# A two-layer decoder trunk on one core: norm parameters and embedding inputs loaded from GpSimd's queue

## The chip, the cores and the metric

The kernel runs on one core of one Trainium2 chip. The metric is the device time of one execution in microseconds; the lower the better. The core has five engines with a queue of instructions each: TensorE (PE in the profile, with its weight loads as PEld), VectorE (DVE), ScalarE (ACT), GpSimd (POOL) and SyncE (SP), which here only issues loads and stores.

## The reference

Two layers over 512 tokens of width 1024 in float32. Layer 0 mixes tokens with a Mamba-2 SSD, layer 1 with an HGRN2; then both do the same:

```python
def sq_relu_mlp(h, w1, w2):
    a = jax.nn.relu(h @ w1)
    return (a * a) @ w2
...
h = layer_norm(DEEPNORM_ALPHA * x + mix, ln_g[i, 0], ln_b[i, 0])
h = layer_norm(DEEPNORM_ALPHA * h + sq_relu_mlp(h, mlp_w1[i], mlp_w2[i]), ln_g[i, 1], ln_b[i, 1])
x = h + jax.nn.sigmoid(h @ ple_w_gate[i]) * (p[i] @ ple_w_proj[i])
```

`w1` is 1024 x 4096, `w2` 4096 x 1024, `ple_w_gate` 1024 x 1024, and the embedding inputs `p[i]` are 512 x 256.

## The kernel before, in words

All tokens stay on the core. Every large product is made of three matmuls with operands that are split into a high and a low part. A weight of 128x1024 is loaded from SP's queue into one of **three `raw` buffers** (`unit`, L107), ScalarE casts it into a `whi` buffer (L114) and VectorE subtracts that into a `wlo` buffer (L116); there are six of each. The `raw` buffer is free for the next load when VectorE is done.

The MLP runs in five groups (`PERIODS`). Groups 0 to 3 make hidden tiles ("T": 24 matmuls of 128x512, then ReLU at L523 and square at L525 on ScalarE, into tiles `a` and `b` of the pool `w4`, two buffers each). `half_blocks` splits pairs of hidden tiles into blocks (casts L355 on ScalarE, subtractions L356 and sums L360 to L364 on VectorE). Groups 1 to 4 multiply the blocks of the group before by `w2` with Strassen's seven products ("Q", 24 matmuls each) in `block_product`. Some products take weights straight from `raw` buffers, the others sums of four loads that `weight_sums` makes in eight buffers `r` (loads L376, sums L382 to L388). A product fills two PSUM banks, py0 and py1 or two of the pool `pj`, and VectorE adds each to `acc` (L466; in group 4's last products L462, which also sums rows for the norm). In group 4 the order is a11, s3, s2, a22, s1, a12, s4; its norm (`layer_norm`, L204 to L215) follows the fifth and the last product. During groups 1 to 3 `sums_ahead` also prepares gate weights and writes them to `pre`.

At the start of group 4 `norm_blocks` calls `ln_params`, which loads the norm's two rows, broadcast to all partitions, into an `a` and a `b` tile. Then the embedding inputs are loaded into a `raw` buffer (L543), and split by ScalarE (L545) and VectorE (L546) into another `a` and `b` tile; the gate products read these after the MLP. The two mixers' norms call `ln_params` too (`norm`).

A scheduler of the framework sets the order of each engine's instructions, from the program's order and priorities (`tc.high_priority`); buffers go round in that order. A queue works in order, so an instruction that waits for a buffer holds those behind it. The names in the rows: `wlo<-raw,whi` is what is written, then what is read; a number behind a name is the buffer's allocation.

Of the kernel before, what the change touches and what calls it, by code (L numbers as in the profile page):

```python
# [9 lines left out]
F32R = mybir.dt.float32r  # L10
# [5 lines left out]
P = 128  # L16
T = 512
NCH = 4
D = 1024
# [22 lines left out]
def trunk(ctx: ExitStack, tc, a):  # L42
    nc = tc.nc
    pool = lambda name, bufs, **kw: ctx.enter_context(tc.tile_pool(name=name, bufs=bufs, **kw))
    cpool = pool("consts", 1)
    raws = pool("raws", RAWS)
# [4 lines left out]
    w4 = pool("w4", 2)  # L51
# [8 lines left out]
    def nm(s):  # L60
        uid[0] += 1
        return f"{s}_{uid[0]}"

    def mk(p, shape, tag, dt=F32, **kw):
        return p.tile(list(shape), dt, tag=tag, name=nm(tag), **kw)

    def f32(t):
        return t.bitcast(F32)
# [34 lines left out]
    def unit(src, lead=LEAD):  # L103
        n = src.shape[1]
        with tc.high_priority(offset=lead):
            raw = mk(raws, [P, 1024], "raw")
            nc.sync.dma_start(raw[:, :n], src)  # L107
        return split(raw[:, :n], lead)
# [83 lines left out]
    def ln_params(i):  # L192
        g = mk(w4, [P, D], "a")
        b = mk(w4, [P, D], "b")
        nc.sync.dma_start(g, a["ln"][2 * i : 2 * i + 1, :].to_broadcast([P, D]))
        nc.sync.dma_start(b, a["ln"][2 * i + 1 : 2 * i + 2, :].to_broadcast([P, D]))
        return g, b

    def layer_norm(c, gb, sums, junk):
# [74 lines left out]
    def norm(i, junk=lambda: tmp("sg", [P, T])):  # L274

        gb = ln_params(i)
        h_s = Split(8)
        sums = mk(sm, [P, NCH, 2], "lnsum")

        def chunk(c):  # L280
            with tc.high_priority(offset=SOON if c < 2 or i % 2 == 0 else 0):
                marks["norm", i] = layer_norm(c, gb, sums, junk)

        def turned(c):
            marks["turned", i] = transpose_split(acc[:, c, :], h_s, c)

        return h_s, chunk, turned, sums
# [4 lines left out]
    def norm_blocks(i):  # L292

        gb = ln_params(i)
        sums = mk(sm, [P, NCH, 2], "lnsum")
        blk = {n: mk(b8, [P, 2, 4, 256], "b8", F32R) for n in ("a11", "a12", "a22")}
# [128 lines left out]
    def ready(dst, n):  # L425

        us = []
        for u in range(2):
            with tc.high_priority(offset=LEAD):
                hi = mk(whip, [P, 1024], "whi", F32R)  # L430
                nc.sync.dma_start(f32(hi), dst[n, u, 0])
                lo = mk(wlop, [P, 1024], "wlo", F32R)
                nc.sync.dma_start(f32(lo), dst[n, u, 1])
            us.append((hi, lo))
        return us
# [50 lines left out]
    def mlp_and_gate(layer, h_s, last, turns=()):  # L486
# [48 lines left out]
        for g, period in enumerate(PERIODS):  # L535
            if g < 4:
                tiles = hidden(g)
            if g > 0:
                if g == 4:
                    blk, after, turned, sums, later = norm_blocks(2 * layer + 1)  # L540
                    p_s = (mk(w4, [P, 2, T], "a", F32R), mk(w4, [P, 2, T], "b", F32R))
                    praw = mk(raws, [P, 1024], "raw")
                    nc.sync.dma_start(praw, a[f"pT_{layer}"].rearrange("p k t -> p (k t)"))  # L543
                    praw = praw.rearrange("p (k t) -> p k t", k=2)
                    nc.scalar.copy(p_s[0], praw)  # L545
                    nc.vector.tensor_sub(p_s[1], praw, f32(p_s[0]))  # L546
                w = [[[w2[8 * g - 8 + 4 * i + 2 * j + u] for u in range(2)] for j in range(2)] for i in range(2)]
                products = block_product(w, blocks.pop(g - 1), SUMS[g - 1], g == 1, *((after, sums) if g == 4 else ()))
            for n, op in enumerate(period):
                next(tiles if op == "T" else products)  # L550
                if 0 < g < 4 and (op == "Q" or n == 1):
                    next(ahead, None)
                if g == 4:
                    for _ in ahead:
                        pass
# [64 lines left out]
        f = [unit(v) for v in wb[0][0]]  # L620
# [4 lines left out]
        f = [unit(v) for v in wb[1][0]]  # L625
# [8 lines left out]
        f = ready(pre, 2)  # L634
# [9 lines left out]
        f = ready(pre, 1)  # L644
# [4 lines left out]
        f = ready(pre, 3)  # L649
# [5 lines left out]
        f = ready(pre, 0)  # L655
# [7 lines left out]
        f = [unit(v) for v in wb[1][1]]  # L663
# [273 lines left out]
    with tc.manual_schedule(engines={mybir.EngineType.PE}):  # L937
# [8 lines left out]
        for k in range(1, 9):  # L946
            i, j = 2 * k, 2 * k + 1
# [47 lines left out]
    out_project(a["wso"][12:16], ys[3], False, *after, scale=rms_group(3, bank(psm, "pm")), spread=True)  # L995
    begin("mlp0")
    x_s, late = mlp_and_gate(0, h_s, False, [lambda c=c: after[1](c) for c in (2, 3)])
    begin("hgrn")

# [367 lines left out]
    out_project(a["who"][4:8], halves[1], False, *after)  # L1367
    begin("mlp1")
    mlp_and_gate(1, h_s, True)
    phase[1].__exit__(None, None, None)  # L1370

# [118 lines left out]
```

## Time and profile before

| what | value |
|---|---|
| median of 3 runs | 1406.96 us (1405.97 to 1407.67) |
| profiled execution: its own time, its span | 1406.46 us, 1404.7 us |
| granted TensorE clock | 1.00 |
| busy: PE, PEld | 1397.1 us (99%), 1167.6 us (83%) |
| busy: DVE, ACT, POOL | 1078.4 us (77%), 775.8 us (55%), 2.4 us |
| SP's DMA queue (q1): bytes, share of 16 engines | 196.59 MB, 41.1% |

Times in the rows are microseconds from the span's start. A row of the timeline gives start, duration, engine, line, operation, what is written and read, and in brackets the idle time before it with what ended it; "x2" is two in one row. SPq is SP's DMA queue: its time is that of issuing, not of the transfer.

### The profile page before, as it was taken

What the parts mean: (1) busy time and instruction counts of PE and PEld (TensorE: products, weight loads), DVE (VectorE), ACT (ScalarE), POOL (GpSimd) and SP (SyncE); (2) the same over time, 40 slices, a digit from 0 to 9 for tenths busy, and PEclk for the clock granted to TensorE, in tenths of its full rate; (3) what the DMA queues carried; (4) which work ended last, traced back from release to release, by engine and by line L of the source; (5) the groups of instructions that cost most, each with busy time, mean ns of one, the idle gap of its engine ahead of it and who ended that gap; (6) DMA issues with size and microseconds to landing.
All of it is one profiled execution on the core that took longest, in us unless ns stands there. A gap on an engine that the chain in (4) does not pass through costs nothing.

```text
span 1404.7 us, 20463 instructions
## 1 busy us (share of the span) xinstructions
PE 1397.1 (99%) x7957; PEld 1167.6 (83%) x7957; DVE 1078.4 (77%) x1780; ACT 775.8 (55%) x1165; POOL 2.4 (0%) x11
## 2 busy tenths in 40 slices
PE   9999999999999999999999999999999999999998
PEld 7888888888988888887888888888898888888787
DVE  7998877696867879679885775776785787778886
ACT  7886666573554555455564446465455464544563
POOL 0000000000000000000000000000000000000000
PEclk9999999999999999999999999999999999999999
DMA  8424333323354764653473321222173656646264
GB/s 296 158 99 135 105 106 120 105 91 106 132 183 143 238 219 162 212 194 135 134 288 120 106 91 67 86 94 73 61 255 114 213 177 223 217 151 210 97 243 155
DMA packets 66817, 214.68 MB, mean 153 GB/s; under 512 B 7712, under 2 KB 8352, under 8 KB 66592
## 3 DMA queue, kind: packets, MB, share of 16 engines
q1 hardware_dynamic: 57504, 196.59, 41.1%
q10 hardware_dynamic: 9216, 16.78, 3.3%
q8 instruction: 62, 1.02, 0.3%
q14 instruction: 35, 0.29, 0.1%
HBM read 194.41 MB, written 18.94 MB: 152 GB/s over the span
## 4 chain that ended last, share of the span: by engine, by line
PE 90%; DVE 5%; DMA 2%; ACT 1%; issue 1%; DVEq 0%; ACTq 0%; SPq 0%
PE pj L120 23%; PE pj L122 23%; PE pj L121 23%; PE py L120 5%; PE py L121 5%; PE py L122 5%; DMA r<-in_w 2%; DVE wlo L116 2%; PE py L880 1%; PE py L1147 1%; PE py L882 1%; DVE b L356 1%; DMA raw<-in_w 1%; PE pt L863 0%; DVE acc L466 0%
## 5 line engine op out<-in xcount | busy, mean ns | idle before, releaser
L116 DVE TENSOR_TENSOR wlo<-raw,whi 128x1024 fp32r<-128x1024 f32 x222 | 269.5, 1221 | 170.6 <-ACT whi L114 169.0
L114 ACT CAST whi<-raw 128x1024 fp32r<-128x1024 f32 x222 | 232.7, 1050 | 288.2 <-PE pj L121 147.9
L120 PE MATMUL pj<-b,whi 128*128 128x512 f32 (+1 forms) x1000 | 379.6, 380 | 0.0
L121 PE MATMUL pj<-b,whi 128*128 128x512 f32 (+1 forms) x1000 | 377.3, 377 | 0.0
L122 PE MATMUL pj<-b,wlo 128*128 128x512 f32 (+1 forms) x1000 | 377.3, 377 | 0.0
L122 PEld LDWEIGHTS pj<-b,wlo 128*128 128x128 f32 x1000 | 188.2, 188 | 34.7
L121 PEld LDWEIGHTS pj<-b,whi 128*128 128x128 f32 x1000 | 188.2, 188 | 34.3
L120 PEld LDWEIGHTS pj<-b,whi 128*128 128x128 f32 x1000 | 187.9, 188 | 34.2
L122 PE MATMUL pj<-whi,b 128*128 128x512 f32 x530 | 206.0, 389 | 0.0
L120 PE MATMUL pj<-whi,b 128*128 128x512 f32 x496 | 196.1, 396 | 0.2 <-DVE cv L753 0.2
L121 PE MATMUL pj<-wlo,b 128*128 128x512 f32 x496 | 193.1, 390 | 0.0
L122 PEld LDWEIGHTS pj<-whi,b 128*128 128x128 f32 x530 | 99.5, 188 | 20.7 <-DVE b L1342 0.2
L114 ACT CAST whi<-r 128x1024 fp32r<-128x1024 f32 x64 | 67.2, 1053 | 88.3 <-PE pj L121 67.7
L120 PEld LDWEIGHTS pj<-whi,b 128*128 128x128 f32 x496 | 93.1, 188 | 20.7 <-issue 0.7
L121 PEld LDWEIGHTS pj<-wlo,b 128*128 128x128 f32 x496 | 93.2, 188 | 18.5
L120 PE MATMUL py<-whi,b 128*128 128x512 f32 x256 | 100.5, 393 | 2.2 <-DVE acc L466 2.2
L122 PE MATMUL py<-whi,b 128*128 128x512 f32 x256 | 99.7, 389 | 0.0
L121 PE MATMUL py<-wlo,b 128*128 128x512 f32 x256 | 99.6, 389 | 0.0
L116 DVE TENSOR_TENSOR wlo<-r,whi 128x1024 fp32r<-128x1024 f32 x64 | 77.7, 1219 | 27.6 <-ACT whi L114 26.8
L120 PEld LDWEIGHTS py<-whi,b 128*128 128x128 f32 x256 | 48.1, 188 | 12.8 <-DVE acc L466 3.0
L122 PEld LDWEIGHTS py<-whi,b 128*128 128x128 f32 x256 | 48.0, 188 | 10.1
L121 PEld LDWEIGHTS py<-wlo,b 128*128 128x128 f32 x256 | 48.1, 188 | 9.8
(375 smaller groups left out, 1934.4 us busy)
## 6 DMA issues: line engine op xcount, KB each, us to landing
raw<-in_w SPq DMA_DIRECT2D x112, 512.0 KB, 3.7
r<-in_w SPq DMA_DIRECT2D x64, 512.0 KB, 4.2
raw<-in_wssd SPq DMA_DIRECT2D x38, 512.0 KB, 3.9
a<-csd SPq DMA_DIRECT2D x16, 512.0 KB, 3.7
raw<-in_wso SPq DMA_DIRECT2D x16, 512.0 KB, 3.8
pre<-sg ACTq DMA_DIRECT2D x32, 256.0 KB, 4.8
whi<-pre SPq DMA_DIRECT2D x16, 512.0 KB, 5.4
wlo<-pre SPq DMA_DIRECT2D x16, 512.0 KB, 6.3
```

The lines of the kernel that those rows point to most:

```text
L114: nc.scalar.copy(hi[:, :n], f)
L116: nc.vector.tensor_sub(lo[:, :n], f, f32(hi[:, :n]))
L120: nc.tensor.matmul(out, sh, mh, start=start, stop=False, **kw)
L121: nc.tensor.matmul(out, sh, ml, start=False, stop=False, **kw)
L122: marks["pe"] = nc.tensor.matmul(out, sl, mh, start=False, stop=stop, **kw)
L356: nc.vector.tensor_sub(lo, f, f32(hi))
L880: nc.tensor.matmul(yd[64 * r : 64 * r + 64, sl], xdt[:, c, r, :], m[:, r, sl], start=True, stop=c == 0)
L882: nc.tensor.matmul(yd[64 * r : 64 * r + 64, sl], pv[:, c - 1, r, :], ecs[:, r, (c - 1) * P : c * P], start=False, stop=True,)
L1147: nc.tensor.matmul(ps[r][32 * b : 32 * b + 32, base + n * c : base + n * c + n], kk[r][:, ts], moving(r, 4 * c + b), start=True, stop=True,)
```

## The change

The norm parameters' two loads are issued from GpSimd's queue in place of SP's, for all four norms. The embedding inputs' load is issued from GpSimd's queue too, and the code of that load and its split stands behind the third product of group 4, where it stood at the group's start.

```diff
     def ln_params(i):
         g = mk(w4, [P, D], "a")
         b = mk(w4, [P, D], "b")
-        nc.sync.dma_start(g, a["ln"][2 * i : 2 * i + 1, :].to_broadcast([P, D]))
-        nc.sync.dma_start(b, a["ln"][2 * i + 1 : 2 * i + 2, :].to_broadcast([P, D]))
+        nc.gpsimd.dma_start(g, a["ln"][2 * i : 2 * i + 1, :].to_broadcast([P, D]))
+        nc.gpsimd.dma_start(b, a["ln"][2 * i + 1 : 2 * i + 2, :].to_broadcast([P, D]))
         return g, b
...
                 if g == 4:
                     blk, after, turned, sums, later = norm_blocks(2 * layer + 1)
-                    p_s = (mk(w4, [P, 2, T], "a", F32R), mk(w4, [P, 2, T], "b", F32R))
-                    praw = mk(raws, [P, 1024], "raw")
-                    nc.sync.dma_start(praw, a[f"pT_{layer}"].rearrange("p k t -> p (k t)"))
-                    praw = praw.rearrange("p (k t) -> p k t", k=2)
-                    nc.scalar.copy(p_s[0], praw)
-                    nc.vector.tensor_sub(p_s[1], praw, f32(p_s[0]))
...
             for n, op in enumerate(period):
                 next(tiles if op == "T" else products)
+                if (g, n) == (4, 2):
+                    p_s = (mk(w4, [P, 2, T], "a", F32R), mk(w4, [P, 2, T], "b", F32R))
+                    praw = mk(raws, [P, 1024], "raw")
+                    nc.gpsimd.dma_start(praw, a[f"pT_{layer}"].rearrange("p k t -> p (k t)"))
+                    praw = praw.rearrange("p (k t) -> p k t", k=2)
+                    nc.scalar.copy(p_s[0], praw)
+                    nc.vector.tensor_sub(p_s[1], praw, f32(p_s[0]))
```

SP's queue around the start of group 4 in layer 0, before. `in_pT` is the embedding inputs, `in_ln` the norm parameters; `r` are the loads for sums; raw_5602 and raw_5608 are the weights of the group's product with a11.

```order
L107 DMA raw_5531<-in_w_0 128x1024
L376 DMA r_5589<-in_w_0 128x1024
L376 DMA r_5592<-in_w_0 128x1024
L543 DMA raw_5574<-in_pT 128x1024
L376 DMA r_5596<-in_w_0 128x1024
L376 DMA r_5599<-in_w_0 128x1024
L107 DMA raw_5602<-in_w_0 128x1024
L107 DMA raw_5608<-in_w_0 128x1024
L195 DMA a_5563<-in_ln 128x1024
L107 DMA raw_5808<-in_w_0 128x1024
L107 DMA raw_5814<-in_w_0 128x1024
L196 DMA b_5564<-in_ln 128x1024
```

The same place of SP's queue after the change; the weights of the product with a11 are raw_5596 and raw_5602 here.

```order
L107 DMA raw_5531<-in_w_0 128x1024
L376 DMA r_5583<-in_w_0 128x1024
L376 DMA r_5586<-in_w_0 128x1024
L107 DMA raw_5596<-in_w_0 128x1024
L376 DMA r_5590<-in_w_0 128x1024
L376 DMA r_5593<-in_w_0 128x1024
L107 DMA raw_5602<-in_w_0 128x1024
L107 DMA raw_5808<-in_w_0 128x1024
L107 DMA raw_5814<-in_w_0 128x1024
L107 DMA raw_5848<-in_w_0 128x1024
```

The first of these weights now stands where the embedding inputs stood, ahead of the last two `r` loads. POOL's queue of the same stretch after the change, where before the change stood only the fill:

```order
L548 DMA raw_5708<-in_pT 128x1024
L195 DMA a_5563<-in_ln 128x1024
L196 DMA b_5564<-in_ln 128x1024
L85 MEMSET pad_6410 128x32
```

The embedding inputs now wait for the `raw` buffer that raw_5531 leaves; the norm's two loads wait for the same readers of their buffers as before.

VectorE's queue at the change from group 3 to group 4, before (py_850 and py_851 are the banks py0 and py1 with group 3's last product; pj_5650 is the first bank of group 4's product with s3):

```order
L466 TENSOR_TENSOR acc_94<-pj_5344,acc_94 128x512
L116 TENSOR_TENSOR wlo_5684<-r_5592,whi_5682 128x1024
L466 TENSOR_TENSOR acc_94<-py_850_5096,acc_94 128x512
L466 TENSOR_TENSOR acc_94<-py_851_5097,acc_94 128x512
L116 TENSOR_TENSOR wlo_5714<-r_5596,whi_5712 128x1024
L466 TENSOR_TENSOR acc_94<-pj_5650,acc_94 128x512
L546 TENSOR_TENSOR b_5573<-raw_5574,a_5572 128x1024
```

And after (pj_5644 is that bank, and L551 the split that was L546):

```order
L466 TENSOR_TENSOR acc_94<-pj_5344,acc_94 128x512
L116 TENSOR_TENSOR wlo_5678<-r_5586,whi_5676 128x1024
L466 TENSOR_TENSOR acc_94<-py_850_5096,acc_94 128x512
L466 TENSOR_TENSOR acc_94<-pj_5644,acc_94 128x512
L116 TENSOR_TENSOR wlo_5714<-r_5590,whi_5712 128x1024
L466 TENSOR_TENSOR acc_94<-py_851_5097,acc_94 128x512
L551 TENSOR_TENSOR b_5707<-raw_5708,a_5706 128x1024
```

The addition of py1 has moved two operations back. On TensorE and ScalarE every instruction keeps its place, and layer 1 is changed in the same way. The lines behind L543 are five lower at the moved code and one higher after it.

## The prediction

> **What bounds the kernel now.** I read the engines' shares first, then TensorE's busy time in stretches of 20 us, then who TensorE waits for, and last the rows of each engine around the two places that this showed. In the stretches the columns are the stretch, its length, and the busy time of PE, PEld, DVE, ACT and POOL.
>
> ```profile
> span 1404.7 us, 20463 instructions
> 0.00:20.00 20.00, 18.95 (x133) 15.20 (x134) 13.29 (x30) 12.74 (x24) 0.41 (x5) 1.00 0.82 288
> 660.00:680.00 20.00, 18.94 (x83) 15.34 (x83) 17.41 (x22) 8.43 (x10) 0.00 (x0) 1.00 0.24 80
> 1300.00:1320.00 20.00, 18.86 (x83) 15.28 (x82) 18.29 (x24) 12.31 (x16) 0.00 (x0) 1.00 0.23 78
> 1400.00:1404.70 4.70, 0.65 (x6) 0.45 (x4) 1.28 (x3) 0.00 (x0) 0.73 (x1) 0.99 0.20 68
> PE py L120 <- DVE acc L466: 2.2, 2, 1.1
> ```
>
> TensorE is the bound: outside the start (1.05 us idle) and the tail (4.05 us) it stands still in only two places, 1.06 us at 660-680 and 1.14 us at 1300-1320, once in each layer's MLP. Both are its wait for an accumulation on VectorE (the last row: 2.2 us in 2 waits). Elsewhere a faster queue can give nothing, so the sum is about these two places and what the new queue may break. The rows of PE there:
>
> ```profile
> 647.14 0.39 PE L120 MATMUL pj<-whi,b 128*128 128x512 f32 x1
> 652.58 0.39 PE L120 MATMUL py<-whi,blk 128*128 128x512 f32 x1
> 658.02 0.39 PE L120 MATMUL pj<-whi,blk 128*128 128x512 f32 x1
> 663.01 0.39 PE L121 MATMUL pj<-wlo,blk 128*128 128x512 f32 x1
> 664.46 0.50 PE L120 MATMUL py<-whi,b 128*128 128x512 f32 x1 [1.06 <-DVE acc L466]
> 664.80 0.40 PE L121 MATMUL py<-wlo,b 128*128 128x512 f32 x1
> ...
> 1313.17 0.39 PE L121 MATMUL pj<-wlo,blk 128*128 128x512 f32 x1
> 1314.70 0.50 PE L120 MATMUL py<-whi,b 128*128 128x512 f32 x1 [1.14 <-DVE acc L466]
> ```
>
> At 647.14 and 652.58 start group 3's last two products; at 658.02 starts group 4's product with `s3`, which the program's order puts ahead of the one with `a11`, and at 664.46 that one. It writes the banks py0 and py1, which the product of 652.58 filled, so it waits until VectorE has added py0 to `acc`. A product is 24 matmuls in 5.44 us, 0.227 us apart. The matmul of 664.46 could thus have been issued at 663.01 + 0.227 = 663.24: 1.22 us lost, and 0.11 more by the wider step to 664.80 (0.34). In layer 1: 1314.70 - 1313.40 = 1.30, and as much again for the step. **Together 1.33 + 1.41 = 2.7 us are to be had, and no more.**
>
> Why VectorE is late, by the rows of DVE, ACT and SP's queue:
>
> ```profile
> 649.71 1.23 DVE L116 TENSOR_TENSOR wlo<-raw,whi 128x1024 fp32r<-128x1024 f32 x1 [2.20 <-ACT whi L114]
> 650.85 0.68 DVE L466 TENSOR_TENSOR acc<-pj,acc 128x512 f32<-128x512 f32 x1
> 651.95 1.29 DVE L356 TENSOR_TENSOR b<-b,b 128x512 fp32r<-128x512 f32 x2 [0.42 <-ACT b L355]
> 661.98 0.68 DVE L466 TENSOR_TENSOR acc<-pj,acc 128x512 f32<-128x512 f32 x1
> 662.59 1.22 DVE L116 TENSOR_TENSOR wlo<-r,whi 128x1024 fp32r<-128x1024 f32 x1
> 663.72 1.28 DVE L466 TENSOR_TENSOR acc<-py,acc 128x512 f32<-128x512 f32 x2
> 652.00:664.00 12.00, 11.40 (x51) 9.10 (x49) 12.00 (x17) 9.27 (x12) 0.00 (x0) 1.00 0.21 81
> ...
> 643.83 1.05 ACT L114 CAST whi<-raw 128x1024 fp32r<-128x1024 f32 x1 [1.31 <-DMA raw<-in_w]
> 648.62 1.05 ACT L114 CAST whi<-raw 128x1024 fp32r<-128x1024 f32 x1 [3.22 <-DMA raw<-in_w]
> 651.29 1.14 ACT L355 CAST b<-b 128x512 fp32r<-128x512 f32 x2
> 657.88 1.05 ACT L114 CAST whi<-r 128x1024 fp32r<-128x1024 f32 x1
> 659.16 1.05 ACT L545 CAST a<-raw 128x1024 fp32r<-128x1024 f32 x1 [0.23 <-DVE b L356]
> ...
> 632.54 0.33 SPq L543 DMA_DIRECT2D raw<-in_pT  x1
> 636.59 1.41 SPq L376 DMA_DIRECT2D r<-in_w  x2
> 639.41 5.51 SPq L107 DMA_DIRECT2D raw<-in_w  x2
> 645.20 0.33 SPq L195 DMA_DIRECT2D a<-in_ln  x1
> 646.33 4.95 SPq L107 DMA_DIRECT2D raw<-in_w  x2
> 661.49 0.33 SPq L196 DMA_DIRECT2D b<-in_ln  x1
> 667.89 0.33 SPq L107 DMA_DIRECT2D raw<-in_w  x1
> ```
>
> From 652 to 664 VectorE has no gap (12.00 of 12.00 us), so py0's addition at 663.72 comes as late as the run of work that starts at 651.95. That run starts with the split of the last hidden tile, which ScalarE prepares (651.29) behind the cast of a weight at 648.62, in queue order. And that cast waited 3.22 us for its load. The load is the second of the two issued from 639.41 on: all three `raw` buffers were taken, one of them by the embedding inputs since 632.54, which nobody reads before 659.16.
>
> **The change, part by part.**
>
> *The embedding inputs' place.* They leave SP's queue, and the weight loads of the first product move up one free buffer each: to 632.54 and 639.41, where 639.41 and (639.41 + 5.51 - 0.33 =) 644.59 stand. The `r` loads between keep their times, as they wait for other buffers, so the second weight lands 5.18 us earlier. The embedding inputs take the buffer free at about 644.6, and two loads more are issued, from POOL.
>
> What then holds the cast is its `whi` buffer, which the last hidden tile's product frees; that product ends where the row of 647.14 starts. So the cast goes from 648.62 to about 647.1, **1.5 us earlier**, and what follows it back to back on ScalarE with it: the pair of casts of 651.29 to 649.8, and the split of 651.95, which follows it by 0.66, to 650.45. Ahead of it VectorE has the addition that stood at 650.85, of a bank ready after half the product of 647.14, at 649.86 at the earliest; it occupies 0.61 us (661.98 to 662.59), and with 0.2 us of latency (my estimate) the split starts at 650.7. The run starts 1.25 to 1.5 us earlier. Inside it, the cast at 657.88 can't come earlier than its buffer, which the product of 652.58 frees at three quarters of its second half, 652.58 + 18 x 0.227 = 656.7; that allows 1.2 us. Its reader is on VectorE only later, so the run holds.
>
> py0's addition moves from 663.72 to 662.2-662.5. PE started 0.74 us behind it (664.46 - 663.72), so it could at 662.95-663.2: the matmul is ready at 663.24 anyway. Layer 0's 1.33 us go in full, with under 0.3 us to spare. In layer 1 the stall is 0.08 longer, so up to 0.05 is left. **Sum: -2.7 us.**
>
> *The order on VectorE.* py1's addition now comes two operations later than directly behind py0's. By the moved times: py0 at 662.5, then 0.61 + 1.14 (662.59 to 663.72) and its own, so py1 starts at 664.8 and is done at 665.5. PE needs py1 after half a product, at 663.24 + 2.72 = 665.96. 0, with 0.45 us to spare. Another few splits swap places at 610-616, without a wait of PE near.
>
> *Norm parameters.* All eight loads go from SP to POOL, whose queue holds nothing between them but a few small fills. In the MLP `b` waits as before for a buffer of the same run, so 661.49 - 1.3 = 660.2; SP stood there until 661.49, with only a load behind it that waits for the embedding inputs' buffer anyway (667.89, now 1.3 earlier). That is why it gives 0. First reads, of a mixer's norm and of the MLP's:
>
> ```profile
> 332.76 0.33 SPq L196 DMA_DIRECT2D b<-in_ln  x1
> 353.44 1.28 DVE L215 SCALAR_TENSOR_TENSOR acc<-acc,lnrs,b 128x1024 f32<-128x1024 f32 x1
> 688.76 1.28 DVE L214 SCALAR_TENSOR_TENSOR acc<-acc,lnmv,a 128x1024 f32<-128x1024 f32 x1
> raw<-in_pT SPq DMA_DIRECT2D x2, 512.0 KB, 3.3
> acc<-in_x SPq DMA_DIRECT2D x1, 2048.0 KB, 8.5
> 725.45 0.99 POOL L1009 MEMSET sc<- 128x512 f32 x2 [385.41 <-DVE b L307]
> 725.25 0.68 DVE L341 TENSOR_TENSOR b<-b 128x512 f32<-128x512 f32 x1
> ```
>
> The MLP's `b` is read no sooner than 28 us behind its issue (688.76 - 660.2), the mixer's 20.7 us (353.44 - 332.76), and layer 1's mixer leaves more. No row shows a load issued from POOL. From issue to landing I bound it by 3.3 us (these bytes from SP) and 8.5 us (the slowest kind of the kernel) and take 5. The embedding inputs, issued at 644.6, are wanted by ScalarE at 659.16 - 1.3 = 657.9: 13.3 us of cover, enough by both ends. The work of issuing may also slow VectorE; the only rows where both work are the last two: beside POOL's fill the VectorE operation took 0.68 us, as every one of its size above. So 0; the other end is 0.73 us for a transfer (POOL's longest operation, in the row of 1400-1404.7).
>
> The Trainium skill, "DMA: Bandwidth & Descriptors", section "Issuing engines are not separate DMA queues", says that loads from any engine run on the same 16 DMA engines, and that another issuer saves only the time of issuing. By that alone the sum would be 0, not 2.7. The trace agrees on the ten issues (0.33 us each, all hidden); here the gain is to come from the buffer and the place in the queue, of which that rule does not speak.
>
> **The rivals.**
>
> *Nothing moves.* Something else holds the run of VectorE back, say the cast's own buffer for over 1 us more. For it: the times above lie close. Against: ScalarE's row names the load. Both stalls stay: 1406.96.
>
> *Half of it comes back.* The load of `b` is issued at 660.2, just as VectorE works without a gap towards py0. If issuing holds VectorE up by 0.73 us, and under 0.3 are to spare, 0.5 to 0.7 us of each stall return: 2.7 - 1.3 = 1.4 us saved, 1405.6. The rows of 725 speak against it. The Trainium skill, "SBUF — State Buffer", section "SBUF: two separate sides", has a rule in this direction: VectorE and GpSimd share a port pair, and some VectorE operations lock GpSimd out, so that a load issued there waits for its descriptors. By that rule the load would be late rather than VectorE; no run here shows it yet.
>
> *Slower: the embedding inputs come late.* ScalarE's cast of them stands in order ahead of the last two casts that VectorE needs before py0. Landing later than 13.3 us after the issue, each us is one us more on PE, in each layer. At 13.3 + 1.4 = 14.7 us the gain is gone, at 16.1 us the kernel is 0.2% slower; at 20 us it would be 1406.96 - 2.7 + 2 x 6.7 = 1417.7. Against it: 14.7 us is nearly twice the slowest load in the trace. For it: VectorE's gapless run from 651, if that can hold the issue up.
>
> **How the numbers follow.** The profiled execution took 1406.46 us, 1.76 outside the span and 0.50 under the median of 1406.96; it becomes 1403.8, the median 1406.96 - 2.7 = 1404.2. Chances: forecast 0.68, nothing 0.10, half back 0.12, late 0.10. What a measurement here tells from no change is about 0.2%, 2.8 us; the forecast lies on that line, and I split it evenly, so faster 0.34, within 0.34 + 0.22 and a part of the late case, 0.58; slower 0.08. The range reaches down by the runs' scatter (1406.96 - 1405.97 = 1.0) to 1403.2, and up over half back and nothing to 1407.2; only the late case is left out.
>
> **What would show it.** Right: PE's two waits for `acc` L466 gone or under 0.2 us; the second weight's cast at 647.1 waiting for PE, not for a load; py0's addition near 662.4; loads from POOL landing in under 13 us; VectorE's 1024-wide subtraction still 1.22 us. Wrong: ScalarE waiting for the embedding inputs at 658, a VectorE operation stretched at 660, a new wait of PE for py1.

## The result, and the profile after

The changed kernel takes 1403.86 us (median of 10 runs) against 1406.64 us of the kernel before in the same comparison: 2.8 us less, a ratio of 0.9979 with a 95% interval of 0.9971 to 0.9988. The forecast was 1404.2 us. One of the ten executions took 2003.23 us at a granted clock of 0.65; the ratio and its interval are of the other nine. The profiled execution took 1403.20 us, with 1.8 us outside its span.

First the span, TensorE's stretches (stretch, length, busy time of PE, PEld, DVE, ACT and POOL, granted clock, DMA share, GB/s) and the longest of TensorE's waits of the changed kernel:

```profile
span 1401.4 us, 20483 instructions
660.00:680.00 20.00, 20.00 (x89) 16.43 (x88) 16.37 (x21) 8.18 (x9) 0.66 (x2) 1.00 0.30 103
1300.00:1320.00 20.00, 20.00 (x90) 16.39 (x89) 18.51 (x25) 11.91 (x14) 0.53 (x1) 1.00 0.19 70
PE pm L155 <- DVE y L152: 1.1, 1, 1.1
```

Both stretches of 20 us are now full, and the two waits for `acc` are gone from the list. What is left at its top, 1.1 us, lies elsewhere. The rows of PE, ACT and DVE at the first place, and of PE at the second:

```profile
646.64 0.39 PE L120 MATMUL pj<-whi,b 128*128 128x512 f32 x1
662.51 0.39 PE L121 MATMUL pj<-wlo,blk 128*128 128x512 f32 x1
662.74 0.48 PE L120 MATMUL py<-whi,b 128*128 128x512 f32 x1
663.05 0.39 PE L121 MATMUL py<-wlo,b 128*128 128x512 f32 x1
...
1295.54 0.39 PE L120 MATMUL pj<-whi,b 128*128 128x512 f32 x1
1311.63 0.48 PE L120 MATMUL py<-whi,b 128*128 128x512 f32 x1
...
646.62 1.05 ACT L114 CAST whi<-raw 128x1024 fp32r<-128x1024 f32 x1 [2.10 <-PE pj L121]
657.42 1.05 ACT L550 CAST a<-raw 128x1024 fp32r<-128x1024 f32 x1
...
649.57 0.69 DVE L466 TENSOR_TENSOR acc<-pj,acc 128x512 f32<-128x512 f32 x1 [0.64 <-PE pj L122]
650.17 1.28 DVE L356 TENSOR_TENSOR b<-b,b 128x512 fp32r<-128x512 f32 x2
660.25 0.68 DVE L466 TENSOR_TENSOR acc<-pj,acc 128x512 f32<-128x512 f32 x1
660.85 1.21 DVE L116 TENSOR_TENSOR wlo<-r,whi 128x1024 fp32r<-128x1024 f32 x1
661.98 0.68 DVE L466 TENSOR_TENSOR acc<-py,acc 128x512 f32<-128x512 f32 x1
664.31 0.68 DVE L466 TENSOR_TENSOR acc<-py,acc 128x512 f32<-128x512 f32 x1
```

The product that started at 647.14 before starts at 646.64 here. Over the nine profiles of this case this row stands between 646.64 and 648.17, with no order by what was changed, so the 0.50 us are put down to the two executions, and 0.50 is added to compare times in layer 0. What the change does at this place is read without that shift, as the distance from the start of this product to the start of the one with `a11` (the first `py<-whi,b` behind the stall): 664.46 - 647.14 = 17.32 us before and 662.74 - 646.64 = 16.10 us now. In layer 1 it is 1314.70 - 1297.30 = 17.40 before (1297.30 is the `pj<-whi,b` row of before there) and 1311.63 - 1295.54 = 16.09 now. So TensorE gains 1.22 + 1.31 = 2.53 us, and the matmul of 662.74 follows the one ahead by the usual 0.23 us. This distance is the measure for the experiments: 34.72 us over both layers before, 32.19 after.

The queues: SP's and POOL's rows (start, duration, count), then the kinds of load by median time to landing (from issue until the data is there):

```profile
631.90 0.33 SPq L107 DMA_DIRECT2D raw<-in_w  x1
638.81 36.63 SPq L107 DMA_DIRECT2D raw<-in_w  x5
644.10 0.53 POOL L548 DMA_DIRECT2D raw<-in_pT  x1 [304.83 <-DVE wlo L116]
660.02 0.53 POOL L196 DMA_DIRECT2D b<-in_ln  x1 [14.79 <-DVE blk L356]
raw<-in_pT POOLq DMA_DIRECT2D x2, 512.0 KB, 3.6
a<-in_ln POOLq DMA_DIRECT2D x4, 512.0 KB, 4.7
b<-in_ln POOLq DMA_DIRECT2D x4, 512.0 KB, 3.9
```

The weight loads stand at 631.90 and from 638.81 on, where before the embedding inputs and the first weight stood. ScalarE's cast of the second weight now waits for PE (a `whi` buffer), no longer for a load.

### The profile page after: what moved, and what is told of

Its sections match the earlier page's. It is cut to its first block, busy times and chain, and to the rows that moved or that the text cites. A ratio compares the mean times of both kernels' runs of the same rounds, so it can differ in the third digit from the quotient of the medians.

```text
span 1401.4 us, 20483 instructions
## 1 busy us (share of the span) xinstructions
PE 1396.2 (100%) x7957; PEld 1168.0 (83%) x7957; DVE 1078.5 (77%) x1780; ACT 776.2 (55%) x1165; POOL 8.0 (1%) x21
## 4 chain that ended last, share of the span: by engine, by line
PE 99%; DVE 0%; ACT 0%; issue 0%; DVEq 0%
PE pj L120 25%; PE pj L122 25%; PE pj L121 25%; PE py L120 5%; PE py L122 5%; PE py L121 5%; PE py L881 1%; PE py L1148 1%; PE py L883 1%; PE pt L864 0%; PE pt L224 0%; PE pm L155 0%; PE pt L824 0%; PE pt L1317 0%; PE py L1256 0%; PE pm L1317 0%
## 5 line engine op out<-in xcount | busy, mean ns | idle before, releaser
L116 DVE TENSOR_TENSOR wlo<-r,whi 128x1024 fp32r<-128x1024 f32 x64 | 77.8, 1220 | 27.9 <-ACT whi L114 26.6
```

What stands on the lines that cost most here:

```text
L116: nc.vector.tensor_sub(lo[:, :n], f, f32(hi[:, :n]))
```

## The experiments

Two theories were to be told apart. *Buffer*: the embedding inputs held one of three `raw` buffers from 632.5 on, 26.6 us ahead of their reader, and the second weight load waited for a buffer. *Queue*: SP is relieved of ten loads. All comparisons are with runs of the kernel before on the same chip.

**The place alone.** From the kernel before, the embedding inputs' block moves behind the third product, and every load stays on SP.

```diff
             for n, op in enumerate(period):
                 next(tiles if op == "T" else products)
+                if (g, n) == (4, 2):
+                    praw = mk(raws, [P, 1024], "raw")
+                    nc.sync.dma_start(praw, a[f"pT_{layer}"]...)
```

> The embedding inputs are asked for behind the third product, as in the changed kernel, but all ten loads stay on SP's queue. Buffer theory (the second weight load waited because the embedding inputs held one of three `raw` buffers): the weight's cast waits for PE near 646.6 to 647.1 and no longer for a load, both waits of PE for `acc` L466 fall below 0.2 us each, and the time is that of the changed kernel, 2.8 us under the kernel before (ratio 0.998). Queue theory (it helps that SP no longer issues these ten loads): nothing gained, ratio 1.000, both waits of 1.2 to 1.3 us stay. If POOL as issuer costs VectorE something, this kernel is faster than the changed one by up to 1.4 us.

Ratio 0.9975 (0.9965 to 0.9985), 1404.18 us. The cast of the second weight, and PE's product starts at both places:

```profile
647.68 1.05 ACT L114 CAST whi<-raw 128x1024 fp32r<-128x1024 f32 x1 [2.10 <-PE pj L121]
647.70 0.39 PE L120 MATMUL pj<-whi,b 128*128 128x512 f32 x1
663.80 0.48 PE L120 MATMUL py<-whi,b 128*128 128x512 f32 x1
1296.64 0.39 PE L120 MATMUL pj<-whi,b 128*128 128x512 f32 x1
1312.73 0.48 PE L120 MATMUL py<-whi,b 128*128 128x512 f32 x1
```

The distances are 16.10 and 16.09 us, those of the changed kernel. The place alone gives the whole gain.

**The queue alone.** All ten loads on POOL, the embedding inputs at their old place.

```diff
-        nc.sync.dma_start(g, a["ln"]...)       # and b, and praw at its old place
+        nc.gpsimd.dma_start(g, a["ln"]...)
```

> All ten loads go to POOL's queue, but the embedding inputs are asked for at the old place, ahead of the group's products. Buffer theory: the embedding inputs still take the `raw` buffer that comes free near 632.5, so the second weight load is still issued near 644.6, its cast still waits about 3 us for the load, both waits of PE stay at 1.2 to 1.4 us and the time is that of the kernel before within 0.3 us (ratio 1.000). Queue theory: the time of the changed kernel, 2.8 us less (ratio 0.998).

Ratio 0.9994 (0.9985 to 1.0003), 1406.82 us. The load from POOL, the cast, and TensorE's longest wait:

```profile
632.59 0.53 POOL L543 DMA_DIRECT2D raw<-in_pT  x1 [293.21 <-DVE wlo L116]
648.10 1.05 ACT L114 CAST whi<-raw 128x1024 fp32r<-128x1024 f32 x1 [2.90 <-DMA raw<-in_w]
PE py L120 <- DVE acc L466: 2.3, 2, 1.4
```

The load takes the buffer at 632.59 as before, the cast waits 2.90 us for its weight, and both stalls are there (2.3 us in 2 waits). The queue alone cannot be told from no change.

**A buffer of its own.** Place and queue as before; the embedding inputs land in the gate stage's two `sg` tiles, in two halves (the split is in halves too, not shown).

```diff
-                    praw = mk(raws, [P, 1024], "raw")
+                    praws = [tmp("sg", [P, T]) for _ in range(2)]
+                    for k in range(2):
+                        nc.sync.dma_start(praws[k], a[f"pT_{layer}"][:, k])
```

> Place and queue as before the change; only the buffer differs: the embedding inputs land in the two tiles `sg` of the gate stage, which nothing uses yet, in two halves, and no longer in a `raw` buffer. VectorE keeps the order of before around py0 and py1 (py1's addition directly behind py0's). Buffer theory: the two weight loads move up to 632.5 and 639.4, the cast goes to about 647, both waits of PE fall below 0.3 us, 2.4 to 2.8 us less (ratio 0.998). Queue theory: ratio 1.000. A third theory, that the changed order on VectorE (py1's addition two operations later) brings the gain: ratio 1.000, since that order is not changed here.

Ratio 0.9978 (0.9968 to 0.9987), 1404.54 us. The cast, and TensorE's wait for `acc` in the list:

```profile
647.70 1.06 ACT L114 CAST whi<-raw 128x1024 fp32r<-128x1024 f32 x1 [2.10 <-PE pj L121]
PE py L120 <- DVE acc L466: 0.3, 1, 0.3
```

The gain comes with neither the new place nor the new queue, and with py1's addition still directly behind py0's on VectorE. So it is the buffer, and the changed order on VectorE is not needed for it. By the distances, 16.09 and 16.54 us, TensorE gains 2.09 of the 2.53 us. The 0.3 us of waiting that stay in layer 1 fit a chain with nothing to spare; what causes them was not followed.

**Two buffers held.** The same two halves, each in a `raw` buffer.

```diff
-                    praw = mk(raws, [P, 1024], "raw")
+                    praws = [mk(raws, [P, 1024], "raw")[:, :T] for _ in range(2)]
```

> Place and queue as before; the embedding inputs come in two halves, each in a `raw` buffer of its own, so that they hold two of the three until VectorE has read them near 665. Buffer theory: one buffer is left for the weights, the first weight load moves to about 644.6 and the second waits for the first one's split, to about 651, so its cast is at about 655.5 in place of 648.6 and the work of VectorE behind it 3 to 7 us later: PE waits 3 to 8 us longer in each layer, 6 to 15 us more in all (ratio 1.004 to 1.011). Queue theory: two loads more of 0.33 us on SP, ratio 1.000 to 1.001.

Ratio 1.0025 (1.0015 to 1.0035), 1411.19 us: slower, as the buffer theory says and the queue theory does not, but by 3.7 us where 6 to 15 were expected. Weight loads, cast and wait:

```profile
645.39 0.33 SPq L107 DMA_DIRECT2D raw<-in_w  x1
651.35 6.24 SPq L107 DMA_DIRECT2D raw<-in_w  x2
654.91 1.06 ACT L114 CAST whi<-raw 128x1024 fp32r<-128x1024 f32 x1
PE py L120 <- DVE acc L466: 3.9, 2, 2.0
```

The loads moved as foreseen, to 645.39 and 651.35, and the cast to 654.91. But the scheduler had put the last hidden tile's casts and splits ahead of this cast, so VectorE had other work and only part of the 6 us reached py0. By the distances, 18.72 and 19.25 us, TensorE lost 1.40 + 1.85 = 3.25 of the 3.7 us here. The size was wrong because I moved the load in an order that I took as fixed.

**The norm parameters back on SP.** The changed kernel with `nc.sync` in ln_params.

> The changed kernel with its eight norm-parameter loads back on SP's queue; the embedding inputs stay behind the third product and on POOL. Buffer theory: the norm parameters' queue is worth nothing, so the time of the changed kernel and of the one with the place alone, 2.7 to 3.4 us under the kernel before (ratio 0.998), both waits of PE for `acc` L466 under 0.3 us. If the norm parameters' queue were worth something, part of the gain would be missing here (ratio 0.9985 or above); if the load of `b` from POOL at 660 held VectorE up in the changed kernel, this one would be up to 1.4 us faster.

Ratio 0.9976 (0.9968 to 0.9985), 1403.82 us, and TensorE is busy throughout both places:

```profile
660.00:680.00 20.00, 20.00 (x89) 16.42 (x88) 16.35 (x22) 8.38 (x9) 0.00 (x0) 1.00 0.28 89
1310.00:1330.00 20.00, 20.00 (x89) 16.42 (x88) 16.35 (x21) 8.18 (x8) 0.00 (x0) 1.00 0.31 105
```

The norm parameters' queue is worth nothing that these runs can tell, and their load from POOL takes nothing back.

**The embedding inputs later.** The changed kernel, with three or four loads in a row into the same buffer, each waiting for the one ahead. In both, VectorE and ScalarE keep the order of the changed kernel around the two places.

```diff
-                    nc.gpsimd.dma_start(praw, a[f"pT_{layer}"]...)
+                    for _ in range(3):      # or 4
+                        nc.gpsimd.dma_start(praw, a[f"pT_{layer}"]...)
```

> The changed kernel, but POOL loads the embedding inputs three times in a row into the same buffer, each load waiting for the one ahead; the order of everything else is unchanged. With 3.6 to 4.2 us for each (3.6 us from issue to landing in the changed kernel) the last lands near 656, still ahead of ScalarE's cast at 657.4. Buffer theory with cover of some 13 us: no change against the changed kernel, ratio 0.998 to the kernel before. Theory that issuing from POOL beside VectorE's gapless run holds VectorE up: two issues more stand at about 648 and 652, inside or at the edge of that run, and would bring back up to 0.5 us for each in each layer, ratio 0.9985 to 0.9995.

> The same with four loads in a row: the last lands at 659 to 661, 1.7 to 3.2 us behind the time at which ScalarE's cast of the embedding inputs now starts (657.4), and that cast stands ahead of two casts that VectorE needs before py0's addition. Late theory (each us behind the cover is one us of PE in each layer): 3 to 6 us slower than the changed kernel, 1407 to 1410, ratio 1.000 to 1.002 to the kernel before, and PE waits for `acc` L466 again. If ScalarE or VectorE had room for it, ratio 0.998.

Three loads: ratio 1.0008 (0.9999 to 1.0016), 1408.56 us, 4.7 us above the kernel with one load on the same chip (1403.82; this is the one with the norm parameters on SP, a queue that made no difference). Four: 1.0082 (1.0065 to 1.0100), 1418.55 us, 14.7 us above it. Both were misses: with three loads no change was expected, with four a loss, but of 3 to 6 us. POOL's rows of the second and third of three loads; the time to landing of the second and of the third load, each by itself; DMA's share (last but one) around them; the two casts in both layers:

```profile
649.78 0.53 POOL L549 DMA_DIRECT2D raw<-in_pT  x1 [2.65 <-DMA raw<-in_pT]
656.45 0.53 POOL L549 DMA_DIRECT2D raw<-in_pT  x1 [6.14 <-DMA raw<-in_pT]
...
raw<-in_pT POOLq DMA_DIRECT2D x1, 512.0 KB, 6.4
raw<-in_pT POOLq DMA_DIRECT2D x1, 512.0 KB, 3.6
raw<-in_w SPq DMA_DIRECT2D x2, 512.0 KB, 6.5
648.00:655.00 7.00, 7.00 (x33) 5.79 (x32) 5.78 (x9) 6.19 (x8) 0.53 (x1) 1.00 0.98 340
656.45:660.05 3.60, 3.60 (x18) 2.98 (x17) 3.60 (x7) 1.68 (x2) 0.53 (x1) 1.00 0.42 147
...
660.09 1.05 ACT L551 CAST a<-raw 128x1024 fp32r<-128x1024 f32 x1 [1.14 <-DMA raw<-in_pT]
1311.43 1.05 ACT L551 CAST a<-raw 128x1024 fp32r<-128x1024 f32 x1 [2.37 <-DMA raw<-in_pT]
```

The second load took 6.4 us and not 3.6, while it shared the DMA engines with two weight loads from SP that took 6.5 us by their median: the engines were 98% busy from 648 to 655. The third, issued at 656.45 in the middle of VectorE's gapless run (VectorE busy 3.60 of 3.60 us), took 3.6 us. So the run of VectorE did not hold this load from POOL up; the slow one is the one that met other loads. The Trainium skill, "DMA: Bandwidth & Descriptors", section "Issuing engines are not separate DMA queues", says that loads from every engine run on the same 16 DMA engines and interleave; the trace agrees, with 6.4 and 6.5 us side by side.

The same runs give the price of being late. The casts of four loads, and PE's rows behind them:

```profile
660.85 1.05 ACT L551 CAST a<-raw 128x1024 fp32r<-128x1024 f32 x1 [2.45 <-DMA raw<-in_pT]
1318.67 1.04 ACT L551 CAST a<-raw 128x1024 fp32r<-128x1024 f32 x1 [7.35 <-DMA raw<-in_pT]
666.13 0.50 PE L120 MATMUL py<-whi,b 128*128 128x512 f32 x1 [2.25 <-DVE acc L466]
1323.95 0.80 PE L120 MATMUL py<-whi,b 128*128 128x512 f32 x1 [7.15 <-DVE acc L466]
```

By the distances from product to product, against 16.10 and 16.09 (the starting rows are at 648.17 and 1298.23 with three loads, 647.62 and 1300.55 with four; the ends are at 665.37, 1316.71, 666.13 and 1323.95):

| | cast late by | TensorE lost |
|---|---|---|
| three loads, layer 0 | 1.14 us | 17.20 - 16.10 = 1.10 us |
| three loads, layer 1 | 2.37 us | 18.48 - 16.09 = 2.39 us |
| four loads, layer 0 | 2.45 us | 18.51 - 16.10 = 2.41 us |
| four loads, layer 1 | 7.35 us | 23.40 - 16.09 = 7.31 us |

At these two places each us late is one us lost, to 0.04 us, and nothing is to spare. The medians lie further apart than these sums: 4.7 against 3.5 us with three loads, 14.7 against 9.7 with four. With three loads 1.1 us of the rest are a wait of TensorE in the first 20 us of the profiled execution (1.4 us for ScalarE, L174, where the kernel with one load shows 0.3), far ahead of the edit. With four loads that wait is 0.6 us, and some 4.3 us of the rest are TensorE's clock, told of in the last section.

## Why the prediction was right

Times of layer 0 stand with the 0.50 us added.

- *What holds the cast, and when it comes.* Forecast 647.1, held by the buffer that PE frees: 646.62 + 0.50 = 647.12, and the row names PE. Right.
- *The run of VectorE.* Split at 650.45 to 650.7: 650.67. It stands behind the addition of 649.57, which waits for PE's half product (646.64 + 2.72 = 649.36), so the estimate of 0.2 us of latency came as 0.21, and the run now starts as soon as PE lets it. py0's addition at 662.2 to 662.5: 662.48. Right.
- *PE.* The product with `a11` was to start when its matmul is ready, at 663.24: 662.74 + 0.50 = 663.24. "Under 0.3 us to spare" was an upper bound; by the table above the spare is 0.04 us at most.
- *The sum.* The two gaps were sized 1.22 and 1.30 us, and 1.22 and 1.31 came. The term of the wider step behind the stall (0.11 in each layer) was mis-sized. It is 663.05 - 662.74 = 0.31 us without any stall, against 0.34 before, so only 0.03 in each layer was to be had. The sum should have been 2.6 us, not 2.7. The medians differ by 2.8, but the interval reaches from 1.7 to 4.1 us, so that they come within 0.1 us of the forecast is luck; the rows above carry the mechanism. TensorE also stood still for 0.16 us between 200 and 220, before and after, which "only two places" leaves out.
- *py1's addition, two operations later.* Forecast 664.8: 664.31 + 0.50 = 664.81, and no wait of PE for it. Its cost of 0 was right.
- *Norm parameters at 0.* Right: with them on SP or POOL the ratios are 0.9976 and 0.9979.
- *Loads from POOL.* Taken as 5 us between bounds of 3.3 and 8.5; they took 3.6 to 4.7 in the changed kernel by kind. The cover, 657.42 - 644.10 = 13.3 us in layer 0, was right.
- *Nothing moves* fell with the cast's row. *Half of it comes back* supposed that issuing from POOL slows VectorE: at the issue of 660.02 to 660.55 VectorE's operations of 660.25 and 660.85 took 0.68 and 1.21 us, where 0.68 and 1.22 stood before with no issue beside them. What the Trainium skill, "SBUF — State Buffer", section "SBUF: two separate sides", says on VectorE locking GpSimd out is not shown by any load here: the one issued at 656.45 beside a VectorE without a gap took 3.6 us.
- *The embedding inputs come late* did not happen, but its slope of one us per us in each layer is what the four rows of the table show. The working had the order right and the landing for a quiet queue; loads that meet others needed more (the second load 6.4 and 5.3 us in the two layers with three loads, 5.0 and 7.7 with four).

## What to carry to other kernels

Ask of an early load which buffer it takes and who is next for that buffer, before asking which queue issues it: here the buffer was the whole gain, and the queue nothing. A prefetch that is asked for long ahead of its reader can cost nothing on its queue and still delay others through its buffer: here a weight load by some 5 us, and TensorE by 1.2 to 1.3 us in each layer. And when work is moved up until the next resource holds it, the spare ends there: behind the change each us by which that chain was late was one us of TensorE.

## What was not expected of the hardware

Issuing a load occupied POOL for 0.53 us where SP showed 0.33 us for the same 512 KB.

TensorE's clock fell behind a short stall. One stretch behind each of the two stalls of the kernel with four loads, with the granted clock last but two, and two matmuls of the first:

```profile
667.50:671.00 3.50, 3.50 (x10) 2.72 (x9) 2.60 (x4) 0.00 (x0) 0.00 (x0) 0.51 0.10 15
1324.00:1330.00 6.00, 6.00 (x15) 4.70 (x16) 3.88 (x5) 0.00 (x0) 0.00 (x0) 0.52 0.26 95
668.06 0.63 PE L121 MATMUL py<-wlo,b 128*128 128x512 f32 x1
668.49 0.63 PE L122 MATMUL py<-whi,b 128*128 128x512 f32 x1
```

1.5 us behind a wait of 2.25 us the matmuls stood 0.43 us apart (668.49 - 668.06) and not 0.227, for 3.4 us, at a granted clock of 0.51; behind the wait of 7.15 us for 5.8 us (1323.95 to 1329.78). Eight steps with 0.2 us too much cost 1.6 us in layer 0, and the like 2.7 us in layer 1, on top of the waits. Yet with three loads a wait of 2.23 us had no such effect. The Trainium skill, "TensorE: Matmul & The Clock Gate", section "Part 1: The HAM clock gate (the "warmup" mystery)", tells of a clock that halves after an idle window of about 3.4 us, in windows that run freely. The halving and the length of the slow stretch in layer 0 agree with it; that 2.25 us of waiting were enough does not.

The times at which the granted clock changes narrow this down. With four loads they are 667.59, 671.00, 1319.54 and 1329.78, so 3.41, 648.54 and 10.24 us lie between them: 1, 190 and 3 times 3.413 us. With three loads the clock is recorded as full from 4.57 to 1407.45, 411 times that. If these are edges of windows that run on by themselves, the wait of 2.25 us lay nearly whole in one window (664.18 to 667.59, in which TensorE was busy for 1.46 us), and the halving came at its end. The wait of 2.23 us was cut by an edge at 1315.29, and TensorE was busy for 2.60 and 1.99 us of the two windows. So the idle share of a window would decide, and not the length of the wait; these two waits fit that, and the share at which the clock halves was not measured.

The 1.2 us stalls of the kernel before were followed by no slow step, so the change gained nothing there.
